# A hybrid decoder layer on one core: another order of the input projection's units, a third buffer for one convolution tile

## The chip, the cores and the metric

The kernel runs on one core of one Trainium2 chip. The metric is the device time of one execution in microseconds. The kernel before was timed in three runs: 1637.55, 1638.69 and 1640.89 us, a median of 1638.69. The profile is of one further execution.

## The reference

One decoder layer is computed in float32 for 1024 prompt positions and 8 x 8 sample positions (1088 columns), with a width of 1024:

```
xn = RMSNorm(x)
[q | k | v | glu_a | glu_b | gate_a | gate_b] = xn @ w_in
A = sliding-window attention(q, k, v; window 128, 16 heads, 4 kv heads, sinks) @ w_o_attn
B = silu(LayerNorm(causal depthwise conv31(glu_a * sigmoid(glu_b)))) @ w_pb
h = x + (sigmoid(gate_a) * A + sigmoid(gate_b) * B) @ w_out
y = h + ConvFFN(RMSNorm(h))        final RMSNorm on y
```

It also returns the last keys, values and convolution rows.

## The kernel before

**Units.** The input projection is done in 44 units. A unit is a block of 128 output channels over all 1088 columns: three column chunks (384, 384, 320), eight steps k of the contraction, and three matmuls a step (`mm3`, L206), since each float32 operand is split in a high and a low part: high x high, high x low, low x high (L208, L209, L210). That is 72 matmuls. The units have letters: `b` and `a` are the two halves of the convolution's gated input of one tile of 128 channels (eight tiles, 0 to 7), `g` a block of one of the gates (16), `q0` and `q1` the queries of head pair 0 and 1 (four each), `k0` and `k1` the keys, and two `v` the values, which are done together. Their order is the table `SEQUENCE` (L62); the weights are packed and loaded in the same order (`weight_order`, L89). Positions in it are counted from 0 here.

**Weights.** SP loads a weight (`wraw<-wall`, L157) into one of two raw buffers. `w_parts` (L165) then splits it: ACT casts the high part (L179) and writes its negative (L180), and a DMA that POOL issues adds the raw weight to it in flight (`wlo<-wraw`, L181), which leaves the low part. `stream` (L212) calls `weight` (L196) with `ahead`, the number of weights that are split beyond the current one. From the output projection on the low part comes from DVE instead (L190).

**Convolution tiles.** A `b` unit begins with `u_start` (L748): a buffer `u` of the pool `cv` (two of them) is cleared at its edges by POOL (L750, L751) and SP loads the cached rows (L752). ACT copies the products into it (L764), then applies the sigmoid (L769). DVE multiplies the products of the `a` unit in (L774). Then the convolution of the tile follows on DVE (`conv`, L570): some 44 multiply-adds (L582), some of them on ACT's and POOL's side products, and closing steps (L601 to L604). Its priority is put behind other work by `CONV_LATER`. POOL issues the stores of the result to a DRAM buffer `d_c` (L605, L606).

**Attention.** It is in two head pairs. Each pair has eight blocks (units) of 128 queries with two head groups, and four sample units. Their steps (`values`, `scores`, `turn`, `mix`) are planned in ticks: one tick is one step k of a chunk, three matmuls. Pair 0 is planned after `v`, pair 1 after the last `q1`. `plan_units` (L881) spaces the units by `SPACING`; `A_TURN` and `A_MIX` say how many ticks after its start the turn and the mix of a unit come, and `FIRST_UNIT` adds ticks to these from the first unit on. `scores` (L440) makes the scores (L449, L450), ACT copies them, DVE masks them (L454) and reduces and inverts for the softmax (L414, L418). `turn` (L457) transposes the probabilities on TensorE (L461), splits them into a high part `pth` (ACT) and a low part `ptl` (DVE, L244), and, but for the first block, DVE multiplies both with a mask (L471). `mix` multiplies with the values (L482).

**LayerNorm.** At position 42 (`LAST_GATES` = 2 units before the end) what is left of attention is drained, its pools close, and SP loads the attention's output `ah`, `al` (L1018, L1019) for the output projection. At position 43, the last unit, the steps of the LayerNorm (`ln_steps`, L608) are planned for four pairs of column blocks. For pair 0: at tick 0 SP loads `ct<-d_c` (L634), at tick 1 DVE adds the channel tiles up (L620), at tick 17 TensorE takes the mean (L628), DVE subtracts it (L644), ACT squares (L647) and DVE adds up again, and at tick 36 TensorE takes the second mean (L628) and the result is applied. The loads read what all eight convolutions have stored. In the same stretch SP loads the gates back (`ga<-d_ga`, L1064) and ACT takes their sigmoid (L1065).

A scheduler orders each engine's instructions by priority when the kernel is built; on the chip each engine runs its list in order, and so do the issues of each DMA queue.

Of the kernel before, what the change touches and what calls it, by code (L numbers as in the profile page):

```python
# [6 lines left out]
F32 = mybir.dt.float32  # L7
F32R = mybir.dt.float32r
AF = mybir.ActivationFunctionType
ALU = mybir.AluOpType  # L10
AX = mybir.AxisListType

P = 128
# [12 lines left out]
WIN = 128  # L26
# [4 lines left out]
UW = PW + NB * SROW  # L31
# [28 lines left out]
FIRST = 5  # L60
LAST_GATES = 2
SEQUENCE = (  # L62
# [3 lines left out]
).split()  # L66
OUT_TAIL = 4
LAST_WEIGHT = 153
# [16 lines left out]
TURN_SOONER = -60  # L85
LN_AT = ((0, 1, 17, 36), (2, 37, 50, 80), (60, 81, 103, 134), (90, 135, 152, 183))
LEAD = (0, 0)
FIRST_UNIT = (10, 6)
SPACING = ({"u": 22, "s": 13}, {"u": 19, "s": 13})  # L89


# [38 lines left out]
class Build:  # L130
# [291 lines left out]
    def attn_unit(self, p, blk, st):  # L422
        nc = self.nc
        q, kd, kl = st["q"], st["kd"], st["kl"]
        qs = slice(blk * P, (blk + 1) * P)
        first = max(blk - 1, 0) * P
        keys = slice(first, first + 2 * WIN)
        own = slice(WIN, 2 * WIN) if blk else slice(0, WIN)
        live = [{}, {}]
        vals = {}  # L430

        def values():
            vt = vals["vt"] = self.t(self.at, [P, 2, 4, HD], "vt", F32R, bufs=2)
            self.split_ps(vt[:, 0, 0:4:3, :], vt[:, 0, 1:3, :], self.v[:, blk, p])
            if blk:
                d = self.t(self.at, [P, 2, HD], "vd")
                nc.vector.tensor_tensor(d, self.v[:, blk - 1, p], self.v[:, blk, p], ALU.subtract)
                self.split_ps(vt[:, 1, 0:4:3, :], vt[:, 1, 1:3, :], d)

        def scores(g):  # L440
            pt = live[g]["pt"] = self.t(self.at, [P, 4, WIN + 4], "p", bufs=2)
            hd = 4 * (2 * p + g)
            nc.gpsimd.tensor_copy(pt[:, :, WIN:WIN + 1], self.c("sink", hd, 4)[:, :, None])
            above = self.masks[:, 0:WIN].bitcast(mybir.dt.uint32)[:, None, :]
            for jj in range(2):
                ps = self.bank("aux").rearrange("p (a b) -> p a b", a=2)
                for j in range(2):
                    h = 2 * jj + j
                    nc.tensor.matmul(ps[:, j, :], q[g][:, h, qs], kd[g][:, keys], start=True, stop=False)  # L449
                    nc.tensor.matmul(ps[:, j, :], q[g][:, h, qs], kl[g][:, keys], start=False, stop=True)  # L450
                two = pt[:, 2 * jj:2 * jj + 2, 0:WIN]
                nc.scalar.copy(two, ps[:, :, own])
                other = ps[:, :, 0:WIN] if blk else self.least[:, None, :].to_broadcast([P, 2, WIN])
                nc.vector.copy_predicated(two, above.to_broadcast([P, 2, WIN]), other)  # L454
            self.band_softmax(pt)

        def turn(g):  # L457
            pt = live[g]["pt"]
            ps = self.bank("aux")
            for h in range(4):  # L460
                nc.tensor.transpose(ps[:, h * P:(h + 1) * P], pt[:, h, 0:P], self.ident)  # L461
            ph = self.t(self.at, [P, 512], "pth", F32R)
            pl = self.t(self.at, [P, 512], "ptl", F32R)
            parts = [(0, ph), (0, pl)]
            with self.later(TURN_SOONER if self.now - self.gated <= 3 else 0):
                self.split_ps(ph, pl, ps)
                if blk:
                    below = self.masks[:, None, WIN:2 * WIN].to_broadcast([P, 4, WIN])
                    for x, tag in ((ph, "pth0"), (pl, "ptl0")):
                        x0 = self.t(self.at, [P, 512], tag, F32R)  # L470
                        nc.vector.tensor_tensor(x0.rearrange("p (a b) -> p a b", a=4),  # L471
                                                x.bitcast(F32).rearrange("p (a b) -> p a b", a=4), below, ALU.mult)
                        parts.append((1, x0))
            live[g]["parts"] = parts

        def mix(g):
            r, o = [slice(x * HD, (x + 1) * HD) for x in (g, 1 - g)]
            av = self.bank("aux")
            parts = live[g]["parts"]
            for n, (y, x) in enumerate(parts):  # L480
                v = vals["vt"][:, y, 2 * g:2 * g + 2, :].rearrange("p x d -> p (x d)")
                nc.tensor.matmul(av, v, x, start=n == 0, stop=n == len(parts) - 1)  # L482
            if g == 0:
                live[0]["t"] = self.t(self.at, [P, 4 * P], "av").rearrange("p (a b) -> p a b", a=4)
            t = live[0]["t"]
            av = av.rearrange("p (a b) -> p a b", a=4)
            nc.scalar.copy(t[r], av[o])
            nc.vector.tensor_tensor(t[r], av[r], t[r], ALU.add)
            if g == 1:
                self.split_ps(q[0][:, :, qs], q[1][:, :, qs], t)  # L490
            if p == 0 and g == 1 and blk in (3, 7):
                b0 = (blk - 3) * P
                self.attn_spill(st, slice(b0, b0 + 4 * P))

        steps = [(A_VALUES, values)]
        for g in range(2):
            steps.append((A_SCORE[g], lambda g=g: scores(g)))
            steps.append((A_TURN[g], lambda g=g: turn(g)))
            steps.append((A_MIX[g], lambda g=g: mix(g)))
        return steps  # L500
# [229 lines left out]
    def phase_x(self):  # L730
        nc, tc, a, pool = self.nc, self.tc, self.a, self.pool
# [13 lines left out]
        def u_views(u):  # L745
            return u[:, PW:].rearrange("p (b t) -> p b t", b=NB)

        def u_start(i):  # L748
            u = self.t(self.cv, [P, UW], "u", bufs=2)
            nc.gpsimd.memset(u[:, 0:HIST], 0.0)  # L750
            nc.gpsimd.memset(u[:, HIST + SEQ:PW], 0.0)  # L751
            nc.sync.dma_start(u_views(u)[:, :, 0:HIST], a["cbT"][i])  # L752
            return u
# [30 lines left out]
        def do_b(i):  # L784
            u = u_start(i)
            self.stream(("b", i), xs, b_evac(u))
            gate_u(u)
            self.gated = self.now
            return u
# [45 lines left out]
        def do_k(p):  # L835
            st = states[p]
            st["ks"] = self.t(kv, [P, NS], "ks")
            st["kd"] = [self.t(kv, [P, SEQ], f"kd{g}", F32R) for g in range(2)]
            st["kl"] = [self.t(kv, [P, SEQ], f"kl{g}", F32R) for g in range(2)]

            def ev(c, o, n, ps):
                m = min(n, SEQ - o)
                for g in range(2):
                    r, x = [slice(y * HD, (y + 1) * HD) for y in (g, 1 - g)]
                    kd = st["kd"][g][:, o:o + m]
                    nc.scalar.copy(kd[r], ps[r, :m])
                    kl = st["kl"][g][:, o:o + m]
                    nc.vector.tensor_tensor(kl[r], ps[r, :m], kd[r].bitcast(F32), ALU.subtract)
                    nc.scalar.copy(kd[x], ps[r, :m])
                    nc.scalar.copy(kl[x], kl[r].bitcast(F32))  # L850
                if m < n:
                    nc.scalar.copy(st["ks"], ps[:, m:n])
                    kf = self.t(gl, [P, 384], "gt", bufs=2)[:, :WIN]
                    nc.scalar.copy(kf, ps[:, m - WIN:m])
                    nc.gpsimd.dma_start(a["o_kp"][p], kf)
                    nc.gpsimd.dma_start(a["o_kn"][p], st["ks"])

            self.stream(("k", p), xs, ev)

        def do_v():  # L860
            ws = [self.weight(("v", 0)), self.weight(("v", 1))]
# [19 lines left out]
        def plan_units(p):  # L881
# [5 lines left out]
            for kind, n in todo:  # L887
                new = self.attn_unit(p, n, st) if kind == "u" else self.sample_unit(p, n, st)
                wait = 0 if steps else FIRST_UNIT[p]
                steps += [(at + d + wait * (d >= A_TURN[0]), f) for d, f in new]  # L890
# [19 lines left out]
        xr[2] = self.norm1_load(p0, 2)  # L910
        nc.sync.dma_start(self.consts[:, rest:], a["consts"][:, rest:])
        u = u_start(0)
        a_t = self.t(self.cv, [P, T], "c")
        self.scale = None
# [21 lines left out]
        bufs = [self.t(self.cv, [P, SEQ // 2 + 15], "sm"), self.t(self.cv, [P, SEQ // 2 + 1], "bt")]  # L936
# [69 lines left out]
        for n, (kind, i) in enumerate(self.order[:self.n_in]):  # L1006
# [18 lines left out]
            if kind == "b":  # L1025
                u = do_b(i)
# [1197 lines left out]
```

## Time and profile before

| what | us |
|---|---|
| median of three runs | 1638.69 |
| lowest, highest | 1637.55, 1640.89 |
| profiled execution, its own time | 1639.45 |
| its span in the trace | 1637.7 |
| TensorE (PE) busy | 1621.8 (99%) |
| VectorE (DVE) busy | 1369.8 (84%) |
| ScalarE (ACT) busy | 901.9 (55%) |
| mean granted TensorE clock | 0.998 |

Times in the trace count from the start of the span. A row of a timeline gives the start, the duration, the engine, the line, the operation, output and inputs, and in brackets the idle time before it with what ended it. A row of the waits gives who waited, for whom, and the microseconds in total, the number of waits and the longest. DVE's share is an average: it is nearly full in some stretches of the input projection and half empty in others.

### The profile page before, as it was taken

The page shows a single profiled execution, that of the slowest core. Times are in us where ns is not written, and L with a number is a line of the kernel's source. Part 1 is how long each engine was busy: PE and PEld are TensorE (multiplying, and loading weights), DVE is VectorE, ACT ScalarE, POOL GpSimd, SP SyncE. Part 2 cuts the span into 40 slices and gives each one's busy share as a digit, 9 for nine tenths or more (in the row PEclk, how much of TensorE's full clock was granted, in tenths as well). Part 3 has the DMA queues.
Part 4 walks back from the last instruction along what each step waited for, and adds up shares of the span by engine and source line. Part 5 has one row for each costly group of instructions (what it writes and reads, how often), then busy time and mean ns, then how long its engine had stood idle before and what let it go on. Part 6 is the DMA issues. An engine that isn't in the chain of part 4 may idle for free.

```text
span 1637.7 us, 30023 instructions
## 1 busy us (share of the span) xinstructions
PE 1621.8 (99%) x11428; PEld 1602.6 (98%) x11428; DVE 1369.8 (84%) x2463; ACT 901.9 (55%) x1948; POOL 301.6 (18%) x587
## 2 busy tenths in 40 slices
PE   9999999999999999999999999999999999999998
PEld 9999999999999999999999999999999999999998
DVE  7889678999869996788755999988888877889767
ACT  6535387875588754576532465555555555524322
POOL 0210122333112221111102422322222111000000
PEclk9999999999999999999999999999999999999999
DMA  6343433545433366548763632344444334676423
GB/s 211 98 98 90 114 95 97 140 132 143 109 85 78 118 215 202 176 154 232 188 227 102 209 119 72 112 116 118 119 120 109 106 106 157 225 177 160 110 62 110
DMA packets 110329, 221.51 MB, mean 135 GB/s; under 512 B 26600, under 2 KB 57320, under 8 KB 110168
## 3 DMA queue, kind: packets, MB, share of 16 engines
q1 hardware_dynamic: 81528, 131.47, 26.0%
q0 software_dynamic: 28224, 87.71, 20.2%
q8 instruction: 90, 1.47, 0.4%
q14 instruction: 55, 0.45, 0.1%
q10 hardware_dynamic: 432, 0.40, 0.1%
HBM read 137.55 MB, written 64.03 MB: 123 GB/s over the span
## 4 chain that ended last, share of the span: by engine, by line
PE 80%; DVE 8%; DMA 4%; issue 4%; ACT 3%; POOL 0%; SPq 0%; POOLq 0%; DVEq 0%; ACTq 0%
PE mm L208 19%; PE mm L209 19%; PE mm L210 19%; PE aux L210 6%; PE aux L208 6%; PE aux L209 6%; DVE c L582 2%; PE aux L482 1%; DVE bt L582 1%; DVE q L824 1%; PE aux L461 1%; PE aux L449 1%; PE aux L450 1%; DMA ct<-d_c 1%; DMA wlo<-wraw 1%
## 5 line engine op out<-in xcount | busy, mean ns | idle before, releaser
L208 PE MATMUL mm<-xh,whi 128*128 128x384 f32 (+1 forms) x904 | 299.2, 331 | 0.2 <-ACT xh L297 0.2
L209 PE MATMUL mm<-xl,whi 128*128 128x384 f32 (+1 forms) x904 | 296.4, 328 | 0.4 <-DVE xl L298 0.4
L210 PE MATMUL mm<-xh,wlo 128*128 128x384 f32 (+1 forms) x904 | 296.3, 328 | 0.3 <-DMA wlo<-wraw 0.3
L209 PEld LDWEIGHTS mm<-xl,whi 128*128 128x128 f32 x904 | 170.5, 189 | 2.5 <-DVE xl L298 0.9
L208 PEld LDWEIGHTS mm<-xh,whi 128*128 128x128 f32 x904 | 170.5, 189 | 2.0 <-ACT xh L297 0.7
L210 PEld LDWEIGHTS mm<-xh,wlo 128*128 128x128 f32 x904 | 170.2, 188 | 1.1 <-DMA wlo<-wraw 0.7
L1470 DVE SCALAR_TENSOR_TENSOR acc<-st,fc,acc 128x1104 f32<-128x1104 f32 x88 | 119.8, 1364 | 12.2 <-issue 6.7
L582 DVE SCALAR_TENSOR_TENSOR bt<-u,consts,bt 128x513 f32<-128x513 f32 x120 | 89.6, 746 | 3.7 <-ACT bt L592 3.1
L210 PE MATMUL mm<-th,wlo 128*128 128x272 f32 x320 | 92.3, 289 | 0.0
L209 PE MATMUL mm<-tl,wlo 128*128 128x272 f32 x320 | 92.3, 288 | 0.0
L208 PE MATMUL mm<-th,wlo 128*128 128x272 f32 x320 | 92.2, 288 | 0.0
L582 DVE SCALAR_TENSOR_TENSOR c<-sm,hsum,c 128x512 f32<-128x512 f32 x120 | 89.3, 745 | 0.5
L210 PE MATMUL mm<-mh,wlo 128*128 128x272 f32 (+4 forms) x304 | 88.9, 292 | 0.0
L582 DVE SCALAR_TENSOR_TENSOR c<-u,consts,c 128x512 f32<-128x512 f32 x112 | 83.4, 744 | 0.4
L243 ACT CAST whi<-wraw 128x512 fp32r<-128x512 f32 x76 | 47.5, 625 | 62.7 <-PE aux L210 25.7
L1815 ACT COPY st<-mm 128x272 f32<-128x272 f32 (+2 forms) x132 | 43.5, 348 | 54.0 <-PE mm L210 53.8
L243 ACT CAST wlo<-wraw 128x512 fp32r<-128x512 f32 x76 | 47.3, 623 | 40.1 <-DVE wraw L1666 16.6
L1468 ACT ACTIVATE acc<-st,fc 128x1104 f32<-128x1104 f32 x44 | 57.6, 1315 | 14.9 <-DVE st L1771 11.8
L208 PE MATMUL aux<-mh,whi 128*128 128x272 f32 (+4 forms) x216 | 63.8, 295 | 0.0
L209 PE MATMUL aux<-ml,whi 128*128 128x272 f32 (+4 forms) x216 | 63.5, 294 | 0.0
L244 DVE TENSOR_TENSOR wlo<-wraw,wlo 128x512 fp32r<-128x512 f32 x76 | 52.7, 695 | 9.5 <-ACT wlo L243 9.3
L208 PEld LDWEIGHTS mm<-th,wlo 128*128 128x128 f32 x320 | 60.2, 188 | 0.0
(726 smaller groups left out, 5799.2 us busy)
## 6 DMA issues: line engine op xcount, KB each, us to landing
wraw<-wall SPq DMA_DIRECT2D x118, 512.0 KB, 3.8
wlo<-wraw POOLq DMA_DIRECT2D x37, 512.0 KB, 4.5
bw<-d_b SPq DMA_DIRECT2D x42, 272.0 KB, 3.9
d_b<-gd POOLq DMA_DIRECT2D x36, 272.0 KB, 6.1
d_b<-acc POOLq DMA_DIRECT2D x24, 272.0 KB, 4.7
ar<-wdn SPq DMA_DIRECT2D x32, 192.0 KB, 3.8
d_g<-acc POOLq DMA_DIRECT2D x10, 544.0 KB, 4.7
ga<-d_ga SPq DMA_DIRECT2D x8, 544.0 KB, 5.4
```

Source lines behind the costliest of these rows:

```text
L208: mm(ps, wh, xh, start=first, stop=False, skip_group_check=more)
L209: mm(ps, wh, xl, start=False, stop=False, skip_group_check=more)
L210: self.last_mm = mm(ps, wl, xh, start=False, stop=last, skip_group_check=more).ins
L243: self.cast = self.nc.scalar.copy(h, src).ins
L244: self.low = self.nc.vector.tensor_tensor(l, src, h.bitcast(F32), ALU.subtract).ins
L449: nc.tensor.matmul(ps[:, j, :], q[g][:, h, qs], kd[g][:, keys], start=True, stop=False)
L450: nc.tensor.matmul(ps[:, j, :], q[g][:, h, qs], kl[g][:, keys], start=False, stop=True)
L461: nc.tensor.transpose(ps[:, h * P:(h + 1) * P], pt[:, h, 0:P], self.ident)
L582: mac = lambda o, x, w: nc.vector.scalar_tensor_tensor(o, x, w, o, ALU.mult, ALU.add)
L1468: nc.scalar.activation(acc, st[:, 0:AW], AF.Identity, bias=fb(f), scale=fw(f, 0))
L1470: nc.vector.scalar_tensor_tensor(acc, st[:, k:k + AW], fw(f, k), acc, ALU.mult, ALU.add)
L1815: self.evicted = (add if second and n == 0 and j == 1 else op)(d, r(banks[bank, j]))
```

## The change

There are five edits. The table `SEQUENCE` is written anew:

```
position   before                                after
0 to 15    b a g g g q0 q0 b a q0 q0 k0 b a v v  b a g g g q0 b a q0 q0 b a q0 k0 v v
16 on      g b a g b a g g g b a                 b a g b a g b a g b a
27 on      q1 k1 q1 q1 q1 b a g b a g*7          q1 k1 q1 q1 q1 b a g*10
```

Tile 1's `a` unit stands at position 7 in place of 8, tile 2's at 11 (13), tile 3's at 17 (18), tile 4's at 20 (21), tile 5's at 23 (26), tile 6's at 26 (33) and tile 7's at 33 (36). The second head pair's queries and keys keep positions 27 to 31, and `k0` now stands directly ahead of `v`. Ten gates stand at the end, where seven stood. The other edits:

```
-FIRST_UNIT = (10, 6)
+FIRST_UNIT = (10, 12)
+THIRD = 6
...
-            ph = self.t(self.at, [P, 512], "pth", F32R)
-            pl = self.t(self.at, [P, 512], "ptl", F32R)
-            parts = [(0, ph), (0, pl)]
+            x = self.t(self.at, [P, 2, 512], "pt", F32R)
+            parts = [(0, x[:, y]) for y in range(2)]
             with self.later(TURN_SOONER if self.now - self.gated <= 3 else 0):
-                self.split_ps(ph, pl, ps)
+                self.split_ps(x[:, 0], x[:, 1], ps)
                 if blk:
-                    below = self.masks[:, None, WIN:2 * WIN].to_broadcast([P, 4, WIN])
-                    for x, tag in ((ph, "pth0"), (pl, "ptl0")):
-                        x0 = self.t(self.at, [P, 512], tag, F32R)
-                        nc.vector.tensor_tensor(x0.rearrange("p (a b) -> p a b", a=4),
-                                                x.bitcast(F32).rearrange("p (a b) -> p a b", a=4), below, ALU.mult)
-                        parts.append((1, x0))
+                    below = self.masks[:, None, WIN:2 * WIN].to_broadcast([P, 8, WIN])
+                    x0 = self.t(self.at, [P, 2, 512], "pt0", F32R)
+                    nc.vector.tensor_tensor(x0.rearrange("p y (a b) -> p (y a) b", a=4),
+                                            x.bitcast(F32).rearrange("p y (a b) -> p (y a) b", a=4), below, ALU.mult)
+                    parts += [(1, x0[:, y]) for y in range(2)]
...
-            u = self.t(self.cv, [P, UW], "u", bufs=2)
+            u = self.t(self.at, [P, UW], "u") if i == THIRD else self.t(self.cv, [P, UW], "u", bufs=2)
...
-            self.stream(("k", p), xs, ev)
+            self.stream(("k", p), xs, ev, ahead=1 + (self.order[self.w_used + 1][0] == "v"))
```

Pair 1's turn and mix come six ticks later than they did; the buffer `u` of tile 6 is one of its own in the pool `at`; the two masking multiplies of 512 columns are one of 1024; and at a `k` unit that stands ahead of `v` two weights are split ahead and not one.

How this moves instructions is shown at three places. The first is DVE at the end of the input projection, where the last convolution's rows end before (`c_5836` is its running sum, `u_5426` its buffer, `ct` what the LayerNorm loads):

```order
L582 SCALAR_TENSOR_TENSOR bt_5838<-u_5426,consts_77,bt_5838 128x513
L582 SCALAR_TENSOR_TENSOR c_5836<-sm_5837,hsum_87,c_5836 128x512
L601 TENSOR_SCALAR u_5426<-c_5836,consts_77 128x64
L602 TENSOR_TENSOR c_5836<-c_5836,bt_5838 128x512
L604 TENSOR_TENSOR u_5426<-c_5836,bt_5838 128x512
L603 TENSOR_TENSOR u_5426<-c_5836 128x512
L190 TENSOR_TENSOR wlo_877_6885<-wraw_6791,whi_876_6884 128x1024
L620 TENSOR_TENSOR u_6892<-ct_6889 128x544
```

After, attention's last mixes (`av`, `q`) stand there, and the LayerNorm's adds behind them:

```order
L487 TENSOR_TENSOR av_6525<-aux_6547,av_6525 64x512
L245 TENSOR_TENSOR q_477_4303<-av_6525,q_476_4302 128x4x128
L245 TENSOR_TENSOR q_477_4303<-aux_6608,q_476_4302 64x4x16 x2
L619 TENSOR_TENSOR u_6804<-ct_6801 128x544
L619 TENSOR_TENSOR u_6804<-u_6804 128x272
L619 TENSOR_TENSOR sm_6805<-u_6804 128x136
L619 TENSOR_TENSOR u_6809<-ct_6801 128x544
L191 TENSOR_TENSOR wlo_817_6797<-wraw_6703,whi_816_6796 128x1024
L619 TENSOR_TENSOR u_6809<-u_6809 128x272
L619 TENSOR_TENSOR u_7009<-ct_6816 128x544
L619 TENSOR_TENSOR sm_6805<-u_6809 128x136
```

The last convolution's closing steps have left this place; they stand some 34 rows further ahead, between attention's steps. The sum `sm_6805` has the first add of the next pair (`ct_6816`) ahead of its last add.

The second place is SP's queue in the last two units, before (`wraw` is a weight load, `ga` a gate's load):

```order
L1019 DMA al_6784<-d_al_58 128x4x320
L157 DMA wraw_6791<-wall 128x1024
L1064 DMA ga_7020<-d_ga_60 128x1088
L1064 DMA ga_7149<-d_ga_60 128x1088
L157 DMA wraw_6882<-wall 128x1024
L634 DMA ct_6889<-d_c_59 128x8x136 x2
L634 DMA ct_6904<-d_c_59 128x8x136 x2
```

And after:

```order
L1018 DMA al_6696<-d_al_58 128x4x320
L158 DMA wraw_6703<-wall 128x1024
L633 DMA ct_6801<-d_c_59 128x8x136
L158 DMA wraw_6794<-wall 128x1024
L633 DMA ct_6801<-d_c_59 128x8x136
L633 DMA ct_6816<-d_c_59 128x8x136 x2
L1063 DMA ga_6932<-d_ga_60 128x1088
L158 DMA wraw_6935<-wall 128x1024
L1063 DMA ga_7061<-d_ga_60 128x1088
```

One half of the first `ct` load stands ahead of the last weight load, the other half behind it, and the gate loads have moved behind both.

The third place is ACT ahead of the `v` units, before (`whi` and `p` are high parts of the two `v` weights, with their negatives `wlo` and `p`; `u` is tile 2's buffer):

```order
L764 COPY u_1636<-mm_1673 128x384
L179 CAST p_1879<-wraw_1728 128x1024
L180 ACTIVATE p_1880<-p_1879 128x1024
L179 CAST whi_160_1730<-wraw_1640 128x1024
L764 COPY u_1636<-mm_1699 128x256
L764 COPY u_1636<-mm_1699 128x8x8
L769 ACTIVATE u_1636<-u_1636 128x1024
L769 ACTIVATE u_1636<-u_1636 128x8x8
L180 ACTIVATE wlo_161_1731<-whi_160_1730 128x1024
```

And after (`q` is the last query unit of pair 0, `kd` are the keys):

```order
L180 CAST p_1773<-wraw_1766 128x1024
L822 ACTIVATE q_28_124<-mm_1701 64x384
L181 ACTIVATE p_1774<-p_1773 128x1024
L822 ACTIVATE q_27_123<-mm_1730 64x256
L180 CAST whi_162_1768<-wraw_1665 128x1024
L181 ACTIVATE wlo_163_1769<-whi_162_1768 128x1024
L822 ACTIVATE q_28_124<-mm_1730 64x256
L829 ACTIVATE qs_125<-mm_1730 64x4x2x8 x2
L845 CAST kd_157_1762<-mm_1778 64x384
```

The two splits stand among the last evictions of the query unit, a whole unit (`k0`) ahead of `v`; before they stood among the evictions of the unit directly ahead of `v`.

6 rows, old and new, of the table SEQUENCE are left out of this document.

## The prediction
> **What bounds the kernel now.** I began with the page's head: is one engine the bound, and how much can be won at all.
>
> ```profile
> span 1637.7 us, 30023 instructions
> PE 1621.8 (99%) x11428; PEld 1602.6 (98%) x11428; DVE 1369.8 (84%) x2463; ACT 901.9 (55%) x1948; POOL 301.6 (18%) x587
> ```
>
> TensorE is busy for 1621.8 of 1637.7 us. The change leaves the number of matmuls as it is, so it can win only from the 15.9 us in which TensorE is idle, and from stretches where it runs slowly. The second view is what TensorE waits for, summed by the line that waits and by the releaser.
>
> ```profile
> PE aux L628 <- DVE sm L620: 4.7, 2, 3.4
> PE mm L209 <- DMA wlo<-wraw: 2.0, 1, 2.0
> PE mm L714 <- DVE least L708: 1.1, 1, 1.1
> PE aux L449 <- DVE ptl L244: 0.6, 1, 0.6
> PE mm L210 <- DMA wlo<-wraw: 0.3, 1, 0.3
> ```
>
> The largest are two waits of the LayerNorm's mean (L628) for DVE's sum (L620), 3.4 and 1.3 us, and one wait of 2.0 us for the low part of a weight. The L714 wait is in the kernel's head, which the change doesn't touch. The third view, TensorE's timeline, places them: the long one is the first mean of LayerNorm pair 0, in the last input unit; pair 0's second mean comes without a wait.
>
> ```profile
> 629.05 1.24 PE L628 MATMUL aux<-sm,mean 128*128 128x272 f32 x2 [3.36 <-DVE sm L620]
> 640.47 0.62 PE L628 MATMUL aux<-sm,mean 128*128 128x272 f32 x2
> 180.31 0.39 PE L209 MATMUL mm<-wlo,xh 128*128 128x256 f32 x1 [2.04 <-DMA wlo<-wraw]
> ```
>
> The fourth view is engine time by stretch: start and end, length, busy time of PE, PEld, DVE, ACT and POOL, granted clock, DMA share, GB/s.
>
> ```profile
> 625.70:629.00 3.30, 0.00 (x0) 0.00 (x0) 1.86 (x5) 0.61 (x2) 0.54 (x1) 1.00 1.11 356
> 629.00:632.50 3.50, 3.45 (x12) 3.25 (x13) 2.58 (x4) 0.34 (x1) 0.54 (x1) 0.51 0.90 323
> 632.50:636.00 3.50, 3.50 (x24) 3.50 (x24) 2.67 (x3) 1.73 (x3) 0.00 (x0) 1.00 0.00 1
> 690.00:693.00 3.00, 1.63 (x10) 1.31 (x9) 1.29 (x4) 0.01 (x1) 0.37 (x1) 1.00 0.52 142
> ```
>
> After the 3.36 us without a matmul the granted clock is 0.51 for 3.5 us: 12 matmuls where the next 3.5 us hold 24. Twelve at the later pace take 12 x 3.5 / 24 = 1.75 us, so 1.75 us are lost on top. The shorter wait near 692 is in a stretch with the clock at 1.00. So the first wait costs 3.36 + 1.75 = 5.11 us. This is the place to look at.
>
> Why is the sum late? DVE's, POOL's and SP's timelines give the chain.
>
> ```profile
> 610.25 0.74 DVE L582 SCALAR_TENSOR_TENSOR bt<-u,consts,bt 128x513 f32<-128x513 f32 x1
> 610.91 0.74 DVE L582 SCALAR_TENSOR_TENSOR c<-sm,hsum,c 128x512 f32<-128x512 f32 x1
> 624.59 0.73 DVE L620 TENSOR_TENSOR u<-ct 128x544 f32<-128x544 f32 x1 [0.84 <-DMA ct<-d_c]
> 628.60 0.30 DVE L620 TENSOR_TENSOR sm<-u 128x136 f32<-128x136 f32 x1
> 639.78 0.29 DVE L620 TENSOR_TENSOR sm<-c 128x136 f32<-128x136 f32 x1
> ```
> ```profile
> 613.92 0.54 POOL L605 DMA_DIRECT2D d_c<-u  x1 [1.26 <-DVE u L603]
> ```
> ```profile
> 606.03 0.85 SPq L1064 DMA_DIRECT2D ga<-d_ga  x2
> 616.75 0.33 SPq L157 DMA_DIRECT2D wraw<-wall  x1
> 620.37 3.88 SPq L634 DMA_DIRECT2D ct<-d_c  x4
> ```
> ```profile
> SPq L634 <- DMA d_c<-u: 3.2, 1, 3.2
> ```
>
> The last convolution (tile 7) ends on DVE near 613.5; its result is stored at 613.92; SP is past the weight load at 616.75 + 0.33 = 617.08 and then waits 3.2 us for that store to land; the four loads follow at 620.37, the adds from 624.59, and the sum is ready at 628.60 + 0.30 = 628.9. It is a chain from the end of the last convolution.
>
> **The change part by part.**
>
> *Convolution inputs sooner.* Units keep their 72 matmuls, and attention stays tied to ticks, so a position in the sequence keeps its time. Tile 6's a unit moves from position 33 to 26, tile 7's from 36 to 33. The ends of those positions are the starts of the next ones, 27 and 34; the third row below is the last product of tile 7 now, and the windows show DVE in two stretches.
>
> ```profile
> 381.20 0.34 PE L208 MATMUL mm<-xh,whi 128*128 128x384 f32 x1
> 473.14 0.34 PE L208 MATMUL mm<-xh,whi 128*128 128x384 f32 x1
> ```
> ```profile
> 525.02 0.56 DVE L774 TENSOR_TENSOR u<-mm,u 128x256 f32<-128x256 f32 x2
> ```
> ```profile
> 440.00:470.00 30.00, 29.42 (x188) 28.47 (x187) 14.37 (x31) 27.15 (x77) 3.59 (x9) 1.00 0.40 105
> 525.00:560.00 35.00, 35.00 (x224) 33.44 (x223) 33.89 (x71) 27.55 (x85) 9.47 (x17) 1.00 0.38 101
> ```
>
> Tile 6 is ready near 381 and not 473, tile 7 near 474 and not 525. From 440 to 470 DVE now idles for 30 - 14.37 = 15.6 us, with no convolution to do; later it is full (33.89 of 35). Convolution work that fills the hole brings the end forward by up to 15.6 us: from 613.5 to 598 at the latest, and sooner, because in the new order some 30 attention rows stand on DVE behind the last convolution step, where now the last 30 convolution steps stand behind attention. Its store then lands before SP reaches the loads near 606, and the 3.2 us wait goes.
>
> What is late next? SP's queue. The first half of pair 0's load goes out near 606, where the first ga load goes now. The second half and the next pair's stand behind the weight load at 616.75, so from 617.08, about a microsecond apiece (four took 3.88). A load of nearly that size, and the DMA engines' load there:
>
> ```profile
> ga<-d_ga SPq DMA_DIRECT2D x8, 544.0 KB, 5.4
> ```
> ```profile
> 616.00:620.00 4.00, 4.00 (x27) 4.00 (x26) 0.00 (x0) 1.11 (x1) 0.00 (x0) 1.00 1.01 407
> ```
>
> The second half lands near 617.1 + 5.4 = 622.5 and the third load near 623.5 to 624. DVE's new order has the third load's first add ahead of the last add of the sum; so the sum is ready after about 624 + 0.73 + 0.30 = 625 plus the weight split and the fold that come between, by hand 626.4. TensorE arrives at 625.7: 0.7 us. Bounds are 0 (all landed in time) and 3.4 (the present wait). With the DMA engines fully taken (1.01) I choose 1.0, near the lower end: three of the four steps of the chain are earlier.
>
> Then the second mean. From the first mean (629.05) to DVE's last sum (639.78 + 0.29 = 640.07) the chain takes 11.02 us; TensorE needs 640.47 - 629.05 = 11.42, but 1.75 of that was the slow clock. At full clock it needs 9.67, and the chain is late by 11.02 - 9.67 = 1.35, say 1.4 us. It could be nothing, if work between its steps moves away, or 2.5, if the gate loads, now behind the ct loads on SP, hold ACT's sigmoids in front of the squares by another microsecond.
>
> So this part is -3.36 - 1.75 + 1.0 + 1.4 = -2.7 us. A wait of 1.0 or 1.4 is shorter than the 3.36 that ended in a slow stretch and near the one at 692 that didn't, so I add no slow restart. [...]
>
> *The v weights.* The wait at 180.31 is for v's weight pair, both of which are needed at once.
>
> ```profile
> 169.24 1.05 ACT L179 CAST p<-wraw 128x1024 fp32r<-128x1024 f32 x1 [5.29 <-DMA wraw<-wall]
> 171.29 1.03 ACT L179 CAST whi<-wraw 128x1024 fp32r<-128x1024 f32 x1
> ```
> ```profile
> 175.08 0.87 POOL L181 DMA_DIRECT2D wlo<-wraw  x1 [2.35 <-ACT wlo L180]
> ```
>
> The second accumulate goes out at 175.08, and TensorE starts 5.2 us later, when it has landed. With k0 directly ahead of v and one more weight split ahead, both casts stand on ACT in front of k0's evictions. That is 2 to 5 us earlier: 2 if the raw buffer that the second v weight needs comes free as late as now (the cast at 169.24 waited 5.29 us for that load), 5 if not. So the last accumulate has landed at 175 to 178.3; it is needed at 180.31 - 2.04 = 178.27. Gain 2.04, bounds 0 and 2.04; I take all of it, since even the late end just does.
>
> *One masking op for two, the turn's tile merged, six ticks more.* The merged multiply needs less of DVE, which is not the bound; counted at nothing. The six ticks (18 matmuls at 29.42 / 188 = 0.16 us in the stretch from 440: 2.8 us) give the second pair's softmax more time before its turn and mix; the 0.58 us wait at L449 for ptl goes (bounds 0 and 0.58). The ah/al loads of the first unit after attention start as much later and are needed only by the output projection.
>
> *What is new.* Four more activation table loads on ACT by the order, each like this one:
>
> ```profile
> 638.18 1.28 ACT L382 ACT_TABLE_LOAD   x1
> ```
>
> ACT is 27.15 us busy of 30 at its fullest here; 1.28 us at a time may show as a late eviction. Nearest rows for such small waits are the 0.3 and 0.6 of the list: I put 0.5, bounds 0 and 3.
>
> The sum: -2.7 - 2.04 - 0.58 + 0.5 = -4.8 us. The profiled execution took 1639.45 us (span 1637.7 and 1.75 around it), which gives 1634.6. It lies 0.76 above the median of the runs, 1638.69, so the forecast in those terms is 1633.9.
>
> **The rivals.**
>
> *The LayerNorm wait only changes its releaser.* ah/al go out 2.8 us later, the DMA engines are full, and the ct loads land 3 us after my estimate; then the 3.36 and the slow clock stay and only 2.04 + 0.58 - 0.5 = 2.1 us are won: 1636.6. For it: share 1.01 at 616 to 620. Against: the first load moves ten microseconds forward. It includes the case that the change does not do what it says, with the convolution's end still late; against that stands the new order itself.
>
> *DVE becomes the bound* (slower). After the hole is filled, the second pair's softmax shares DVE with two convolutions from 447 on; between its 18th and 19th reduction the order puts 18 convolution steps where none stood, 18 x 0.66 us (610.25 to 610.91) = 11.9 us. Against: the hole offers 15.6 us and the six ticks 2.8. If attention is late all the same, by more than 3 us at two places, TensorE stalls and restarts slowly at 5.1 each: 1633.9 + 10.2 = 1644.1. It decides from two such stalls on.
>
> *b5 waits for its buffer* (slower). b5 moves to position 22, into the buffer of tile 3's convolution.
>
> ```profile
> 331.33 0.54 POOL L605 DMA_DIRECT2D d_c<-u  x1 [2.27 <-DVE u L604]
> 334.40 0.14 POOL L750 MEMSET u<- 128x30 f32 x1
> ```
> ```profile
> 325.45 0.33 PE L208 MATMUL mm<-xh,whi 128*128 128x384 f32 x1
> ```
> ```profile
> 307.35 0.68 DVE L414 TENSOR_REDUCE nm<-p 128x4 f32<-128x516 f32 x1
> ```
>
> Now that buffer is free at 334.40. TensorE, with four banks, can go on until its fifth chunk, near 325.45. Kept, that is 9 us and 1.75: 1633.9 + 10.7 = 1644.6. Against: the order puts that convolution's end ahead of the 11th reduction (307.35), so the store lands near 313. It decides if the convolution ends after about 322: the store takes 334.40 - 331.33 = 3.1 us to land.
>
> **How the numbers follow.** About 0.2% (3.3 us) is what a measurement of this kernel can tell from no change: 1635.4 and 1642.0. Forecast 0.64; LayerNorm wait kept 0.26; DVE the bound 0.06; buffer 0.04. The first is faster, the second the same, the last two slower: 0.64, 0.26, 0.10. Lower end: no residual at either mean and no new wait, 1633.9 - 1.0 - 1.4 - 0.5 = 1631.0, and the 1.3 of pair 1's mean gone too: 1629.7. Upper end: the rival at 1636.6, with the upper bounds of the small waits (3 and not 0.5): 1639.1. Beyond it lie the slower cases.
>
> **What would show it.** Right: the L628 wait falls from 3.4 to under 1.5 and no clock of 0.51 near 629; the store of the last convolution before 600; ct loads without a d_c wait; no wait at v; DVE full in 440 to 470. Wrong: a wait at L628 over 3 us whose releaser is a DMA (first rival), waits at L449, L461 or L482 between 447 and 600 (second), an idle TensorE near 325 (third), or a v wait that stays.

## The result, and the profile after

The changed kernel takes 1646.77 us in the median of five runs (1646.17 to 1649.91), the kernel before 1638.69 beside it. The ratio is 1.0049, with a 95% interval of 1.0035 to 1.0064: slower, by about 8 us, where 4.8 us less was forecast. The profiled execution took 1649.91 us and is the slowest of the five; the text says where that matters. One execution of the experiment first6 (2251.36 us, granted clock 0.654) and one of the kernel before (2644.55 us, 0.556) ran far slower than all others, and the ratios leave them out.

The head of the page after:

```profile
span 1648.1 us, 29986 instructions
PE 1627.5 (99%) x11428; PEld 1606.1 (97%) x11428; DVE 1371.5 (83%) x2435; ACT 909.3 (55%) x1952; POOL 308.1 (19%) x587
```

TensorE's matmuls are as many as before. Its idle time rose from 15.9 to 20.6 us, and its busy time, which should not change, by 5.7; at least a part of that is a slower clock, whose mean over the span fell from 0.998 to 0.996. What TensorE waits for, after:

```profile
PE aux L627 <- DVE sm L619: 4.5, 2, 2.4
PE aux L481 <- DVE pt L245: 1.9, 1, 1.9
PE aux L462 <- ACT p L421: 1.8, 4, 0.7
PE mm L210 <- DMA wlo<-wraw: 1.4, 1, 1.4
PE mm L211 <- DMA wlo<-wraw: 1.0, 1, 1.0
PE aux L481 <- ACT pt L244: 0.9, 1, 0.9
```

The two waits that the change was to remove are still there: the first mean's is 2.4 (3.4 before), the v weight's 1.4 (2.0). New are waits of attention's steps for DVE and ACT (L481 is the mix, L462 the transposes) and one for a weight (L211).

Such a list doesn't say how far behind TensorE is. For that I read from TensorE's timeline when the same unit begins in each kernel. In the table stand the times of the kernel before, and how much later each other kernel is there, in us; the columns are the start of units 22, 32 and 42, of the output projection's first unit, and of its sixth, which lies behind the LayerNorm's pair 1. The kernels below the second line are the experiments.

```
                unit 22   unit 32   unit 42   output 0   output 5
before           302.32    441.44    604.73     634.68     698.55
after             +6.28     +5.55    +10.61      +8.87     +11.24
head_only         -0.20     +0.39     -0.39      +3.50      +2.47
b4_later          +0.32     +1.52     +5.28      +3.59      +3.50
two_tiles         +2.14     +2.55     +7.84      +6.20      +6.13
first6            +4.44     +3.66     +9.21      +4.24      +4.94
light6            +5.46     +4.69     +8.80      +5.75      +6.19
ct_first          +4.81     +4.09     +9.06      +3.29      +2.14
b4_ct             +0.43     +1.60     +5.31      -0.46      -0.54
b4_ct_first6      -0.60     +0.61     +5.64      -0.13      -0.61
one_sig4          +1.58     +3.83     +8.13      +6.54      +5.88
no6               +4.35     +3.62     +3.74      +0.66      +0.84
hold6             -0.11     +1.09     +1.61      -4.17      -0.49
hold6_first6      +0.75     +1.95     +2.40      -1.36      -1.46
```

The changed kernel loses some 5.5 us by unit 32, most of it in units 20 and 21 (unit 20 still starts level, at 270.58 after 270.63), and 5.1 more between units 32 and 42; the LayerNorm gives back 1.7, and its pair 1 takes 2.4 more.

The +6.28 at unit 22 is not all loss. These are units 20 and 21, first after and then before (columns as in the prediction):

```profile
270.58:308.60 38.02, 35.93 (x217) 33.96 (x216) 34.52 (x69) 31.27 (x81) 12.84 (x22) 0.96 0.51 132
270.63:302.32 31.69, 31.69 (x204) 30.70 (x203) 31.32 (x66) 26.89 (x78) 10.03 (x18) 1.00 0.51 147
```

After, 13 more of attention's matmuls stand ahead of unit 22. At 31.69 / 204 = 0.155 us each they take some 2 us, so about 4.3 us are lost in these two units.

**Units 20 and 21.** Engine time by stretch, two rows after, and the second stretch before:

```profile
284.00:288.00 4.00, 3.12 (x20) 2.60 (x19) 3.23 (x10) 3.67 (x7) 2.11 (x4) 1.00 0.48 110
288.00:292.00 4.00, 2.98 (x11) 2.47 (x10) 3.95 (x9) 2.42 (x5) 1.69 (x3) 0.69 1.03 191
288.00:292.00 4.00, 4.00 (x29) 4.00 (x27) 3.97 (x7) 3.99 (x8) 2.72 (x6) 1.00 0.95 338
```

TensorE is idle for 0.9 us of the first and 1.0 us of the second, where its clock falls to 0.69; before, it is busy there all the time, at full clock. ACT's and POOL's timelines say what came late.

```profile
273.79 1.28 ACT L768 ACT_TABLE_LOAD   x1
275.08 1.07 ACT L768 ACTIVATE u<-u 128x1024 f32<-128x1024 f32 x1
276.17 1.28 ACT L417 ACT_TABLE_LOAD   x1
279.13 1.28 ACT L768 ACT_TABLE_LOAD   x1
280.43 0.26 ACT L768 ACTIVATE u<-u 128x64 f32<-128x64 f32 x1
281.76 1.04 ACT L180 CAST whi<-wraw 128x1024 fp32r<-128x1024 f32 x1
286.95 0.57 ACT L244 CAST pt<-aux 128x512 fp32r<-128x512 f32 x1
```
```profile
285.12 0.91 POOL L182 DMA_DIRECT2D wlo<-wraw  x1
```

The same cast of a weight stands in the kernel before at:

```profile
273.16 1.04 ACT L179 CAST whi<-wraw 128x1024 fp32r<-128x1024 f32 x1
```

Tile 4's sigmoid, one unit sooner than before, falls into a softmax of pair 0. Its two instructions stand apart, so the sigmoid's table is loaded twice, and the exponent's once between. The cast of the weight stands behind all of it, at 281.76 and not at 273.16. So the weight's low part goes out at 285.12; TensorE needs it at 288.8 and has it at 289.8. The turn's cast (286.95) is late too, and the mix waits 0.9 us for it.

**Units 32 to 42.** How long ACT waits at pair 1's start, from 440 on (first row after; the row of before, from 436 on, behind it), and the load of the exponent's table with which pair 1's softmax begins, after and before:

```profile
ACT q L822 <- DVE q L823: 6.0, 3, 3.7
```
```profile
ACT q L823 <- DVE q L824: 4.1, 2, 3.0
```
```profile
456.21 1.28 ACT L417 ACT_TABLE_LOAD   x1
```
```profile
447.37 1.28 ACT L416 ACT_TABLE_LOAD   x1
```

That is 456.21 - 446.99 = 9.2 us into unit 32, and was 447.37 - 441.44 = 5.9. In the ten microseconds after 460, TensorE works 7.41:

```profile
460.00:470.00 10.00, 7.41 (x43) 6.16 (x42) 9.97 (x18) 9.29 (x24) 3.50 (x2) 1.00 0.01 2
```

**The LayerNorm.** The timelines of SP and POOL, DVE's first add, a stretch while the first load was under way, and two around the first mean:

```profile
605.79 0.38 SPq L1017 DMA_DIRECT2D ah<-d_ah  x1
617.89 0.38 SPq L633 DMA_DIRECT2D ct<-d_c  x1
626.29 5.97 SPq L633 DMA_DIRECT2D ct<-d_c  x3
```
```profile
573.72 0.85 POOL L604 DMA_DIRECT2D d_c<-u  x1
```
```profile
631.23 0.72 DVE L619 TENSOR_TENSOR u<-ct 128x544 f32<-128x544 f32 x1 [24.57 <-DMA ct<-d_c]
```
```profile
620.00:625.00 5.00, 5.00 (x33) 5.00 (x31) 0.00 (x0) 0.69 (x2) 0.86 (x2) 1.00 1.09 314
635.00:638.20 3.20, 0.79 (x6) 0.49 (x4) 3.20 (x6) 0.00 (x0) 0.00 (x0) 0.92 1.10 379
638.20:641.70 3.50, 3.50 (x14) 3.27 (x15) 2.77 (x4) 1.47 (x2) 0.00 (x0) 0.59 0.82 320
```

The last convolution's store went out at 573.72, 40 us sooner than before, as forecast; SP no longer waits for it. But the first ct load, out at 617.89, feeds its first add only at 631.23, 13.3 us later, while the DMA engines are fully taken (1.09 from 620 to 625). DVE waits 24.6 us for it. The slow clock follows the 2.4 us wait too (0.59 from 638.2 to 641.7).

### The profile page after: what moved, and what is told of

It reads as the page before. It is cut to its first block, busy times and chain, and to the rows that moved or that the text cites. A ratio compares the mean times of both kernels' runs of the same rounds, so it can differ in the third digit from the quotient of the medians.

```text
span 1648.1 us, 29986 instructions
## 1 busy us (share of the span) xinstructions
PE 1627.5 (99%) x11428; PEld 1606.1 (97%) x11428; DVE 1371.5 (83%) x2435; ACT 909.3 (55%) x1952; POOL 308.1 (19%) x587
## 4 chain that ended last, share of the span: by engine, by line
PE 72%; DVE 14%; issue 6%; DMA 4%; ACT 3%; POOL 1%; SPq 0%; POOLq 0%; DVEq 0%; ACTq 0%
PE mm L209 16%; PE mm L211 16%; PE mm L210 16%; PE aux L210 6%; PE aux L209 6%; PE aux L211 6%; DVE c L581 5%; DVE bt L581 2%; PE aux L481 1%; DVE q L823 1%; DMA d_t<-ct 1%; DMA ct<-d_c 1%; PE aux L462 1%; DMA wlo<-wraw 1%; ACT ct L661 1%
## 5 line engine op out<-in xcount | busy, mean ns | idle before, releaser
L211 PE MATMUL mm<-xh,wlo 128*128 128x384 f32 (+1 forms) x904 | 296.6, 329 | 1.0 <-DMA wlo<-wraw 1.0
L211 PEld LDWEIGHTS mm<-xh,wlo 128*128 128x128 f32 x904 | 170.6, 189 | 2.0 <-DMA wlo<-wraw 1.3
L211 PE MATMUL mm<-th,wlo 128*128 128x272 f32 x320 | 92.3, 289 | 0.0
L211 PE MATMUL mm<-mh,wlo 128*128 128x272 f32 (+4 forms) x304 | 88.9, 292 | 0.0
```

The costliest lines, as they stand in the source:

```text
L211: self.last_mm = mm(ps, wl, xh, start=False, stop=last, skip_group_check=more).ins
```

## The experiments

Twelve kernels were run. Theory A names the two places above; B blames the merged tile of the turn; C the six ticks, through ah/al. Each kernel is compared with the kernel before on the same chip, whose medians there were 1638.6 to 1639.4 us.

**head_only: only the head of the new sequence.**

```
-    "b a g b a g b a g b a "
-    "q1 k1 q1 q1 q1 b a g g g g g g g g g g"
+    "g b a g b a g g g b a "
+    "q1 k1 q1 q1 q1 b a g b a g g g g g g g"
```

> Positions 0 to 15 of the sequence and all other edits as in the changed kernel, positions 16 on as before (so tiles 3 to 7 come as late as they did). Theory A (the loss comes where the sooner tiles meet attention: about 5.5 us at 280 to 295, where tile 4's sigmoid lies among pair 0's softmax on ACT, and about 4 us at 446 to 500, where tile 6's convolution lies among pair 1's first units on DVE): both are gone, 1637 to 1640, and the LayerNorm's first wait is back at about 3.4. Theory B (the merged turn tile holds attention up wherever it is tight): still 3 us or more above 1638.7. Theory C (the six ticks end attention later and so send ah/al into the LayerNorm's loads): the first mean waits over 3 us, its releaser a DMA, 1640 or more.

1641.29 us, ratio 1.0014 (1.0005 to 1.0023). Both places are clean (+0.39 at unit 32, -0.39 at unit 42), so it is the sooner tiles 3 to 7 that cause the losses there. At unit 42 it is level; then the first mean waits twice as long as before:

```profile
631.66 1.25 PE L627 MATMUL aux<-sm,mean 128*128 128x272 f32 x2 [6.95 <-DVE sm L619]
```
```profile
595.83 0.38 SPq L1017 DMA_DIRECT2D ah<-d_ah  x1
618.91 7.47 SPq L633 DMA_DIRECT2D ct<-d_c  x4
```

ah goes out at 595.83 where it was 592.24, and the wait grew by 3.6 us. So the losses at the first two places come with the sooner tiles, as A has it, and the wait here is as C has it. B is out: the merged tile is in this kernel, and attention isn't late.

**b4_later: one gate unit ahead of tile 4.**

```
-    "b a g b a g b a g b a "
+    "b a g g b a b a g b a "
```

> The changed kernel with one gate unit moved from behind tile 4 to ahead of it: b4 and a4 stand at positions 20 and 21 in place of 19 and 20 (a4 at 21 is its place in the kernel before), tiles 5 to 7 unchanged. Theory A: the stall near 287 and the slow clock behind it go, the one at 446 to 500 stays: 1641 to 1643. B and C: within 1.5 us of the changed kernel's 1646.8.

1642.11 us, 1.0017 (1.0008 to 1.0027): about 5 us faster than the changed kernel, as theory A had it. Unit 22 is at +0.32 and not +6.28, and TensorE has no wait in units 20 and 21; unit 42 is still 3.8 us later than unit 32.

**two_tiles: the turn's two tiles and two masking multiplies, as before.** The diff of the turn, taken back.

> The changed kernel with the turn's high and low part in two tiles again and two masking multiplies of 512, as before. Theory A: within 1.5 us of 1646.8. Theory B: 3 to 5 us faster, 1642 to 1644, and the waits at the mix (L482 here) for pt are gone. C: unchanged.

1646.67 us, 1.0044 (1.003 to 1.0058). Unchanged within the noise, and the same mix waits for the same step, now by the old name:

```profile
466.03 0.50 PE L483 MATMUL aux<-pth,vt 128*128 128x512 f32 x1 [2.56 <-DVE ptl L245]
```

B falls. In this profile unit 22 is at +2.14 and not +6.28, which is not the tile's doing in the main: fewer matmuls stand ahead of it (206, and 217 in the changed kernel), the clock stays at 1.00, and the one wait in unit 21, 1.87 us for the weight, is as long as the changed kernel's two together (0.88 and 1.02). Under 1 us of the difference is left.

**first6: the six ticks taken back.**

```
-FIRST_UNIT = (10, 12)
+FIRST_UNIT = (10, 6)
```

> The changed kernel with pair 1's turn and mix six ticks sooner, as before. Theory A: more stalls of TensorE at 460 to 485, as the turns come sooner while DVE and ACT are just as late: 1647 to 1650. Theory C: attention ends about 3 us sooner against TensorE, ah/al with it, and the LayerNorm's first wait falls from 2.4 to under 1: 1643 to 1645. B: unchanged.

1644.17 us, 1.0034 (1.0022 to 1.0046): about 2.5 us faster, between what the two theories said. Pair 1's first transposes wait longer, as A said (though the kernel isn't slower); and the first mean doesn't wait at all, as C said.

```profile
459.21 1.35 PE L462 MATMUL aux<-consts,p 128*128 128x128 f32 x4 [3.37 <-ACT p L421]
```
```profile
626.00:629.50 3.50, 3.50 (x23) 3.50 (x22) 1.46 (x3) 2.66 (x3) 0.54 (x1) 1.00 1.09 374
```

So the six ticks help attention a little, and take the LayerNorm's gain away.

**light6: half of tile 6's multiply-adds left out.**

```
-        for j in range(1, 16):
+        for j in range(1, 16 if i != 6 else 8):
```

> The changed kernel, with 22 of the 44 multiply-adds of tile 6's convolution left out (some 14.6 us of DVE), so that DVE is free when pair 1's attention starts. If DVE makes the loss at 446 to 500 (theory A): the waits at L462, L481 and L450 there go, about 4 us faster than the changed kernel, 4 us above the kernel before. If ACT makes it (tile 7's sigmoid with its two table loads stands in the same place): within 1.5 us of the changed kernel, 6.5 or more above the kernel before.

1644.68 us, 1.0042 (1.003 to 1.0055). 1 to 2 us faster than the changed kernel, which decides for neither side: the mix's wait is 0.62 and not 1.91, but unit 42 is still 4.1 us later than unit 32. It is the late half of the convolution that is left out here. The early half kept DVE full up to 463, and the softmax began as late as in the changed kernel (9.2 us into unit 32). The next kernel leaves out the early half too.

**no6: nearly all of them left out.**

```
-        for j in range(1, 16):
+        for j in range(1, 16 if i != 6 else 2):
```

> The changed kernel with all but 3 of the 44 multiply-adds of tile 6's convolution left out, the early ones too (the run that left out the late half kept DVE full up to 463, and the last query splits, which wait for their turn on DVE, were as late as in the changed kernel). If the loss at 446 to 500 begins with these splits: pair 1's first exponent starts about 3 us sooner and 3 to 5 us are won, 3 to 5 above the kernel before. If ACT alone makes it: within 1.5 us of the changed kernel.

1641.2 us, 1.0016 (1.0007 to 1.0025): 5 to 6 us faster than the changed kernel. Between units 32 and 42 nothing is lost (+3.62, +3.74). The last query splits on DVE, and the exponent's table load on ACT:

```profile
448.43 0.42 DVE L823 SCALAR_TENSOR_TENSOR q<-mm,q 64x256 fp32r<-64x256 f32 x1 [0.92 <-ACT q L822]
449.79 0.43 DVE L823 SCALAR_TENSOR_TENSOR q<-mm,q 64x256 fp32r<-64x256 f32 x1 [0.94 <-ACT q L822]
```
```profile
451.46 1.28 ACT L417 ACT_TABLE_LOAD   x1
```

That is 6.4 us into unit 32 (445.06), as good as the 5.9 before. In the changed kernel DVE stands thus instead:

```profile
451.93 0.75 DVE L581 SCALAR_TENSOR_TENSOR c<-sm,hsum,c 128x512 f32<-128x512 f32 x1
452.71 0.42 DVE L823 SCALAR_TENSOR_TENSOR q<-mm,q 64x256 fp32r<-64x256 f32 x1
453.16 0.76 DVE L581 SCALAR_TENSOR_TENSOR bt<-u,consts,bt 128x513 f32<-128x513 f32 x1
453.83 0.75 DVE L581 SCALAR_TENSOR_TENSOR c<-u,consts,c 128x512 f32<-128x512 f32 x1
454.61 0.43 DVE L823 SCALAR_TENSOR_TENSOR q<-mm,q 64x256 fp32r<-64x256 f32 x1
```

These two splits stand behind three and two convolution steps, and ACT's next eviction waits for a split (3.7 us the longest). The late start then carries through pair 1.

**one_sig4: tile 4's small sigmoid left out.**

```
-            for d, *_ in u_part(u, 0, T):
+            for d, *_ in list(u_part(u, 0, T))[:1 + (i != 4)]:
...
```

> The changed kernel, with the sigmoid of tile 4's 64 sample columns left out. In the changed kernel it stands on ACT behind a softmax, and needs a table load for itself and another one back: two loads of 1.28 us and 0.26 us go, 2.8 us of ACT between 276 and 290. If ACT's extra table loads make the stall near 287: it goes, and the time is 4 to 5 us under the changed kernel's, 3 to 4 above the kernel before. If it is the weight's way over POOL and the DMA alone, or DVE: within 1.5 us of the changed kernel, 6.5 or more above the kernel before.

1643.91 us, 1.0028 (1.0016 to 1.0039), some 3 us faster than the changed kernel, less than expected. The weight's cast comes at 279.19, 2.6 us sooner, and one wait of 0.77 is left in unit 21. Unit 22 is at +1.58, with 13 fewer matmuls ahead of it than in the changed kernel. But by unit 32 it is +3.83, no better than first6 or no6, which keep the small sigmoid (+3.66, +3.62): a wait has come at 320.

```profile
287.13 0.44 PE L211 MATMUL mm<-xh,wlo 128*128 128x384 f32 x1 [0.77 <-DMA wlo<-wraw]
320.16 0.33 PE L462 MATMUL aux<-consts,p 128*128 128x128 f32 x1 [1.40 <-ACT p L421]
```

So the extra table loads delay the weight's cast and make part of the loss at tile 4; where the whole 3 us comes from, this profile doesn't show. The rest goes with the tile's place, as b4_later shows, but not step by step. What makes the wait at 320 wasn't tried.

**ct_first: the ct loads of pairs 0 and 1 ahead of ah/al.** The steps of the LayerNorm keep their ticks, only the loads move.

```
+                steps = [s for x in range(KT // 2) for s in self.ln_steps(x)]
...
+                for x in (0, 4):
+                    steps[x][1]()
...
                 for (o, w) in CHUNKS:
                     nc.sync.dma_start(ah[:, :, o:o + w].bitcast(F32), ...
...
```

> The changed kernel with the four loads of the LayerNorm's first two column pairs issued ahead of ah/al, at the start of the last unit but one. Theory C (ah/al, sent after attention's end, keep the DMA engines busy and hold the ct loads up): no wait at the first mean and no slow clock behind it, no wait at pair 1's mean: 4 to 6 us faster than the changed kernel, 2 to 4 above the kernel before. If the output projection then waits for ah/al instead, as much is lost again there: no faster.

1641.92 us, 1.0025 (1.0016 to 1.0034): 4 to 5 us faster than the changed kernel. From unit 42 to the output projection it gains 5.8 (+9.06 to +3.29), near the 5.1 that the first mean and its slow clock cost before, and TensorE is at full clock where its mean was late:

```profile
632.00:636.00 4.00, 4.00 (x26) 3.92 (x25) 1.34 (x1) 2.58 (x3) 0.54 (x1) 1.00 0.47 170
```

**b4_ct and b4_ct_first6: both mends, with and without the six ticks.** The edits of b4_later and ct_first together; the second with FIRST_UNIT at (10, 6).

> Both mends: b4 at position 20 and the ct loads ahead of ah/al. If the two losses are separate places (A and C), they add up: 9 to 11 us faster than the changed kernel, 1 to 3 us faster than the kernel before, with the stall at 446 to 500 left.

> The same without the six ticks. A: the stall at the start of pair 1 is larger (3.4 us at 459 when the six ticks were taken out alone), and the sooner end of attention wins nothing, since the ct loads no longer stand behind ah/al: 0 to 2 us slower than the one with both mends.

1638.13 us, 0.9997 (0.9988 to 1.0006), and 1638.55, 0.9999 (0.999 to 1.0008). The mends add up (8 to 9 us), and give the kernel before its time back, no more: 3.7 us are still lost between units 32 and 42, and 5.0 without the six ticks. Between the two there is no difference that can be measured, though the profiles differ as expected.

**hold6 and hold6_first6: tile 6's convolution behind the last query split on DVE.** Added to the two above. `last_q` is the last query split on DVE, `held` the convolution of tile 6.

```
                 if i == (1, 3):
+                    with tc.issue_after(self.last_q):
+                        self.held()
                     plan_units(1)
```

> Both mends (b4 at position 20, ct loads ahead of ah/al), and tile 6's convolution may not start on DVE before the last query split of pair 1. If the splits' place on DVE makes the loss at 446 to 500: 3 to 4 us faster than with both mends alone, 3 to 4.5 us faster than the kernel before. Against it: the last convolution ends some 10 us later, near 590 to 600, and the ct loads may wait for it: then as fast as both mends alone, or slower.

> The same without the six ticks. With the splits on time the six ticks should not be needed: within 1 us of the one before. If ACT is late by itself at pair 1's start, TensorE waits at L462 near 459 again, 2 to 4 us slower.

hold6: 1638.27 us, 0.9995 (0.9986 to 1.0004), a miss for the time. The loss between units 32 and 42 is gone (+1.09, +1.61). But the last store goes out at 596.31, the ct loads and what follows on SP are later, and the output projection's first weight is late: its split on DVE (629.66) stands ahead of the LayerNorm's centring (630.92), and the second mean waits 2.79 us. hold6_first6: 1636.58 us, 0.9981 (0.9972 to 0.999): faster than both kernels. It loses 0.45 us between units 32 and 42 and gains 3.8 at the LayerNorm. As the last store goes out at 596.97, the ct loads are out only at 605.74, and three of the six ah/al loads go ahead of them; the first mean doesn't wait all the same. Its largest waits are these:

```profile
PE mm L211 <- DMA wlo<-wraw: 1.8, 1, 1.8
PE mm L210 <- DMA wlo<-wraw: 1.2, 1, 1.2
PE aux L631 <- DVE sm L623: 1.1, 1, 1.1
```

## Why the prediction was wrong

Two steps failed: the tiles' sooner sigmoid and convolution were priced at 0.5 us as new small waits and cost some 10 us at two places in attention, and the six ticks' later ah/al loads were called free and cost some 3.5 us at the LayerNorm.

**What bounds the kernel** was right, and so was the chain from the last convolution to the first mean: with the ct loads in time (ct_first, first6) the wait and the slow clock go (the clock is 1.00 there in both).

**The convolution's end** was right: forecast before 598, stored at 573.72.

**The residual at the first mean** was mis-sized: 1.0 us, and it is 2.4 with a slow clock. I priced a ct load at 5.4 us from its neighbours in a list of medians, though the same page showed the DMA engines fully taken there (1.01 from 616 to 620); the first took 13.3. The gain of the LayerNorm's pair 0 is 1.7 us (+10.61 to +8.87), not 2.7, and pair 1's mean lost more than that.

**The six ticks** were the step of the sum that failed at the LayerNorm. I had ah/al leaving 2.8 us later against TensorE and called that free because the output projection needs them late. They do leave that much later (605.79 lies 9.6 us ahead of unit 42's start, 592.24 lay 12.5 ahead). But the ct loads stand behind them in the same queue. I had this in the first rival, at 0.26, as an accident of the DMA engines, and not as a price of the six ticks. head_only and first6 show the price, about 3.5 us each way.

**The new small waits**, 0.5 us with bounds 0 and 3, were the largest error. I saw four more table loads in the order and covered them by ACT's mean load of a stretch; I did not look at which softmax they fall into. The five kernels that have this code in pair 0 (after, first6, light6, ct_first, no6) are 4.4 to 6.3 us late at unit 22; some 2 us of that are attention's matmuls that stand ahead of the unit there (217 or 218, and 204 before), so tile 4 cost 2.6 to 4.3.

**DVE as the bound**, the second rival, at 0.06, came true, at another place than I put it. I counted the convolution steps between softmax reductions and set them against the hole from 440 to 470. But the last query splits pass through that hole: DVE was idle there because it had no convolution, and that was why the splits were prompt. Filling it delays the splits, and with them ACT and the first softmax, by 3.3 us; with the same convolution behind the last split (hold6) only 0.5 us is lost between units 32 and 42. The price, 5.1 us between units 32 and 42, is about that of one stall of the rival, not two.

**The v weights**: 2.04 us forecast, and the wait is 1.4 with 0.3 of a new one behind it, a gain of 0.3. It landed at 179.5, later than the later of the two ends that I gave (178.3), which rested on the raw buffer's coming free as late as before. In the profiles of the experiments, whose units up to `v` are the same, the wait is 0.7 to 1.5.

**The merged tile**, counted at nothing, is nothing (two_tiles). **The third rival**, tile 5's buffer, did not happen: no stall near 325.

In sum the expected gain of some 5 us at the LayerNorm was there (ct_first takes it). It was eaten by the later ah/al, and some 10 us were lost at two places ahead of it, where the sooner tiles' sigmoid and convolution meet attention.

## What to carry to other kernels

Idle time of an engine in front of a chain is slack for that chain: before filling it, list the short steps that pass through it and who waits for each. Work that is moved sooner brings all its engines with it, so follow a tile's ACT function and its table loads to the very softmax that they land in. And a transfer that is needed late still isn't free to move: look at what stands behind it in its queue.

## What the runs showed of the hardware

In these profiles the slow clock was not tied to a long wait. In unit 21, the changed kernel's execution has waits of 0.88 and 1.02 us and then a clock of 0.69; the run first6 has the same code there, with waits of 0.88 and 0.89, and stays at full clock:

```profile
286.00:290.00 4.00, 2.24 (x10) 1.35 (x9) 3.17 (x10) 3.72 (x7) 2.33 (x3) 1.00 1.01 200
290.00:294.00 4.00, 4.00 (x27) 3.86 (x26) 3.19 (x8) 2.45 (x7) 0.19 (x1) 1.00 1.02 175
```

So too at the LayerNorm's pair 1: a wait of 1.37 us before, with the clock at 1.00, and one of 2.06 in the changed kernel, with a clock of 0.51 behind it:

```profile
702.59 1.28 PE L627 MATMUL aux<-sm,mean 128*128 128x272 f32 x2 [2.06 <-DVE sm L619]
```
```profile
703.00:706.00 3.00, 3.00 (x10) 2.77 (x10) 0.80 (x3) 0.49 (x1) 0.54 (x1) 0.51 1.14 335
```

The prediction added no slow stretch behind waits of 1.0 and 1.4 us, since they were shorter than the 3.36 that had ended in one. Here a slow clock stands behind waits of 1.02 and 2.06 us, and the same code in unit 21 ran at 1.00 in one execution and at 0.69 in another; what decides between the two no run shows. One such stretch is worth some 1.5 us here, an estimate from the rows with 0.59 (3.5 us) and 0.51 (3 us), which may be part of the 3 us between the profiled execution and the median.
